# Moving twelve element-wise operations per border from VectorE to GpSimd in an encoder layer

## The chip, the cores and the metric

The kernel runs on one core of one Trainium2 chip. The metric is the device time of one execution in microseconds (us). The engines are named as the profile names them: PE (TensorE matmul), DVE (VectorE), ACT (ScalarE), POOL (GpSimd), SP (SyncE, which issues the loads).

## What is computed

Two sequences of 512 tokens with 1024 features go through one layer of a bidirectional encoder: pooling mixer and attention, a SwiGLU feed-forward network, and a gate for embeddings per layer. Two places matter here, and both have the same form: the hidden state is normed and multiplied by two large matrices or one.

```python
def rms_norm(x, g):
    y = x * rsqrt(mean(x * x, axis=-1) + EPS)
    return y * g
...
u2 = rms_norm(h, ln2)                                     # first border
h = h + (silu(u2 @ w_gate) * (u2 @ w_up)) @ w_down
gate = sigmoid(rms_norm(h, ple_norm) @ w_ple_gate)        # second border
return h + gate * (p @ w_ple_proj)
```

## The kernel before

Activations lie with features on the 128 partitions and the 512 tokens along the free axis, so one feature tile is a 128x512 block of float32. Every product is made of three passes over split operands: `split` (L128 to L133) makes the high part on ACT (L130) and the low part, source minus high part, on DVE or POOL (L133), and `mm3` (L155 to L159) issues high by high (L157), high by low (L158) and low by high (L159).

The two sequences s0 and s1 and the two halves of the features and of the outputs are the 2x2 blocks of a fast matrix product with seven products instead of eight (`seven`). Its seven activation operands are called B11, B21, T1, T2, T4, T3 and B22, four tiles each, and are used in this order. The seven weight operands are made on the fly by `stationary` (L649 on): SP loads raw weights, DVE adds and subtracts (L661), and ACT and DVE split. `fill` keeps up to eight such weights ahead, and SP's next load into a raw buffer waits until DVE has read the old one.

A border is the place where the normed hidden state becomes these operands. The first (gains at G_LN2) stands before the gate and up matrices, the second (G_PLE) before the gate of the embeddings; each begins with four products whose first step needs only B11 and B21. `norm_rows(..., False)` leaves the factors of the rows, `rb`, in a PSUM bank. `normed_first` makes B11 and B21 of s0. `normed_rest` (L765 to L786) does the rest from s1: x12 is the normed first half of s1, x22 its second half; T1 = x12 - x11 (L646), T2 = x22 - T1 (L776), T4 = x21 - T2 (L779), t3 = x22 - x12 (`difference`, L646), and then the pieces of B22 = x22 (L784) and of T3 = t3 (L786). `normed` makes one tile, on the engine that `eng` picks from the table TURNS by a name and an index i; x22 has i = 3:

```python
def normed(q, gc, k, rb, dst, i):                                        # L745
    if eng("norm", i) is nc.vector:
        nc.vector.scalar_tensor_tensor(dst, q.h[k], gcol(gc + k), rb[0], op0=ALU.mult, op1=ALU.mult)
    else:
        nc.scalar.activation(dst, q.h[k], AF.Copy, scale=gcol(gc + k))   # L749
        if len(rb) == 1:
            rb.append(Ft("rb"))
            nc.scalar.activation(rb[1], rb[0], AF.Copy)                  # L752
        nc.gpsimd.tensor_tensor(dst, dst, rb[1], op=ALU.mult)            # L753
```

So on DVE a tile is one instruction that reads `rb` in PSUM (L747); on POOL it is a scaled copy by ACT (L749) and a product of two operands in SBUF (L753), with one copy of `rb` from PSUM to SBUF for each border (L752). The bank of `rb` has the tag g, one of two; the products c and d (the tags of OB) take banks of that tag too, so the next c waits until the last reader of `rb` has ended. The order of the instructions on each engine is set by a scheduler from the order in the program, their dependences and its own estimates; each engine then works through its list in order. T3's pieces have the turn n5, those of B22 n4, the difference t3 the turn t3.

Of the kernel before, what the change touches and what calls it, by code (L numbers as in the profile page):

```python
# [60 lines left out]
    "hlo": "d",  # L61
    "wadd": "d",
    "wlo": "d",
    "norm": "d",
    "n0": "p",
    "n1": "p",
    "n2": "d",
    "n3": "d",
    "n4": "d",
    "n5": "d",  # L70
    "n6": "d",
    "tdif": "d",
    "t3": "d",
    "out": "d",
}
EMB = (1, 8, 4)
# [1030 lines left out]
```

## Time and profile before

| | us |
|---|---|
| median of 3 runs (1181.11 to 1186.27) | 1182.92 |
| the profiled execution, its own time | 1179.86 |
| its span in the trace | 1178.1 |

The span holds all instructions of the profiled execution; 1.76 us of its own time lie around it. The profiled execution is 3.06 us below the median. In the rows below, a row of the timeline is one instruction or several equal ones in a run (x8), with the start, the time from the first start to the last end, and in brackets the idle time of the engine ahead of it with what ended it. In the table by stretch, each engine has its busy time and, in brackets, its number of instructions; PEclk is the granted clock of PE as a share of the full 2.4 GHz.

### The profile page before, as it was taken

Reading aid. Unit: us, or ns where it says so; the run is one execution under the profiler, and the core shown is the slowest. Engines: PE = TensorE matmul, PEld = TensorE weight load, DVE = VectorE, ACT = ScalarE, POOL = GpSimd, SP = SyncE. Lnnn points to the kernel's source line nnn. Section 1 sums busy time; section 2 is a strip of 40 time slices with the busy share of each in tenths; the row PEclk is TensorE's granted clock in tenths of the full one; section 3 lists DMA queues with packets and bytes.
Section 4 is the critical chain, followed back from the end, with each engine's and each line's share of the span. In section 5 each row is a group of like instructions: output and inputs, shape, how many; then the busy total and the mean of one; then the engine's idle time right before and its main releaser. Section 6 shows DMA issues by size and latency. Waiting matters only on the chain.

```text
span 1178.1 us, 14952 instructions
## 1 busy us (share of the span) xinstructions
PE 1131.2 (96%) x5168; PEld 922.0 (78%) x5168; DVE 893.9 (76%) x1639; ACT 584.1 (50%) x1135; POOL 228.2 (19%) x290
## 2 busy tenths in 40 slices
PE   7999999998999989999999999999999999999997
PEld 7898756776778867888888888888778888887775
DVE  7377877778583789987768776787597867885997
ACT  7144478777562535655445454554332222345643
POOL 3533464746100220000000000000322212001200
PEclk9999999998999999999999999999999999999999
DMA  6211100102233521545244433544998475636045
GB/s 220 71 57 53 43 1 1 55 3 88 90 119 114 155 96 54 199 176 183 90 175 179 161 127 124 185 173 153 411 415 333 165 317 198 212 94 220 28 163 186
DMA packets 53644, 173.25 MB, mean 147 GB/s; under 512 B 6208, under 2 KB 6976, under 8 KB 53568
## 3 DMA queue, kind: packets, MB, share of 16 engines
q1 hardware_dynamic: 41328, 127.73, 32.3%
q0 software_dynamic: 12240, 44.57, 9.7%
q8 instruction: 40, 0.66, 0.2%
q14 instruction: 36, 0.29, 0.1%
HBM read 119.33 MB, written 52.95 MB: 146 GB/s over the span
## 4 chain that ended last, share of the span: by engine, by line
PE 81%; DVE 9%; issue 3%; POOL 3%; DMA 2%; ACT 2%; SPq 0%; DVEq 0%; ACTq 0%; POOLq 0%
PE a L158 8%; PE a L159 8%; PE a L157 8%; PE b L157 6%; PE b L158 6%; PE b L159 5%; PE s L523 4%; PE d L158 3%; PE d L159 3%; PE d L157 3%; PE o L157 2%; PE o L158 2%; PE o L159 2%; PE c L157 2%; PE c L158 2%
## 5 line engine op out<-in xcount | busy, mean ns | idle before, releaser
L130 ACT ACTIVATE w<-s 128x512 fp32r<-128x512 f32 (+2 forms) x168 | 96.8, 579 | 162.9 <-DVE s L661 61.5
L157 PE MATMUL a<-u,w 128*128 128x512 f32 x444 | 170.8, 390 | 2.9 <-DVE h L963 2.3
L158 PE MATMUL a<-u,w 128*128 128x512 f32 x444 | 172.9, 389 | 0.2 <-POOL u L133 0.2
L159 PE MATMUL a<-u,w 128*128 128x512 f32 x444 | 170.7, 389 | 0.0
L130 ACT ACTIVATE w<-raw 128x512 fp32r<-128x512 f32 (+2 forms) x126 | 70.8, 577 | 140.7 <-PE a L159 83.9
L133 DVE TENSOR_TENSOR w<-s,w 128x512 fp32r<-128x512 f32 (+2 forms) x168 | 103.8, 624 | 21.8 <-ACT w L130 21.3
L158 PE MATMUL b<-u,w 128*128 128x512 f32 x296 | 116.1, 393 | 4.3 <-DVE u L133 4.3
L157 PE MATMUL b<-u,w 128*128 128x512 f32 x296 | 115.9, 393 | 3.8 <-ACT w L130 2.1
L159 PE MATMUL b<-u,w 128*128 128x512 f32 x296 | 115.6, 392 | 0.0
L157 PEld LDWEIGHTS a<-u,w 128*128 128x128 f32 x444 | 83.2, 188 | 21.9 <-DVE h L963 2.7
L158 PEld LDWEIGHTS a<-u,w 128*128 128x128 f32 x444 | 83.3, 188 | 17.9 <-POOL u L133 0.6
L159 PEld LDWEIGHTS a<-u,w 128*128 128x128 f32 x444 | 83.3, 188 | 17.3
L133 DVE TENSOR_TENSOR w<-raw,w 128x512 fp32r<-128x512 f32 (+2 forms) x126 | 78.7, 637 | 21.1 <-ACT w L130 21.0
L942 POOL DMA_DIRECT2D u<-opT4p x11 | 6.2, 564 | 401.1 <-DVE s L661 363.8
L157 PEld LDWEIGHTS b<-u,w 128*128 128x128 f32 x296 | 56.0, 189 | 17.7 <-ACT w L130 2.9
L158 PEld LDWEIGHTS b<-u,w 128*128 128x128 f32 x296 | 55.9, 189 | 17.2 <-DVE u L133 5.6
L523 PE MATMUL s<-qkT 96*128 96x512 f32 x128 | 63.2, 596 | 2.8 <-ACT p L527 2.5
L159 PEld LDWEIGHTS b<-u,w 128*128 128x128 f32 x296 | 56.0, 189 | 11.5
L157 PE MATMUL c<-u,w 128*128 128x512 f32 x148 | 58.6, 399 | 5.0 <-DVE x L747 5.0
L159 PE MATMUL c<-u,w 128*128 128x512 f32 x148 | 58.4, 395 | 0.0
L158 PE MATMUL c<-u,w 128*128 128x512 f32 x148 | 58.3, 394 | 0.0
L158 PE MATMUL d<-u,w 128*128 128x512 f32 x148 | 57.7, 390 | 0.6 <-DVE u L133 0.6
(238 smaller groups left out, 2739.8 us busy)
## 6 DMA issues: line engine op xcount, KB each, us to landing
raw<-in_w_gate SPq DMA_DIRECT2D x24, 512.0 KB, 4.1
raw<-in_w_up SPq DMA_DIRECT2D x24, 512.0 KB, 3.6
raw<-in_w_down SPq DMA_DIRECT2D x24, 384.0 KB, 3.7
raw<-in_w_o SPq DMA_DIRECT2D x16, 512.0 KB, 3.6
raw<-in_w_pg SPq DMA_DIRECT2D x12, 512.0 KB, 3.7
opB11p<-st SPq DMA_DIRECT2D x11, 512.0 KB, 2.6
opB21p<-st SPq DMA_DIRECT2D x11, 512.0 KB, 3.7
opT1p<-st SPq DMA_DIRECT2D x11, 512.0 KB, 4.4
```

Source lines behind the costliest of these rows:

```text
L130: nc.scalar.activation(hi, src, AF.Copy)
L133: lo_eng.tensor_tensor(lo, src, hi.bitcast(F32), op=ALU.subtract)
L157: nc.tensor.matmul(ps, lhs[0], rhs[0], start=first, stop=False, skip_group_check=more)
L158: nc.tensor.matmul(ps, lhs[0], rhs[1], start=False, stop=False, skip_group_check=more)
L159: nc.tensor.matmul(ps, lhs[1], rhs[0], start=False, stop=last, skip_group_check=more)
L523: nc.tensor.matmul(ps, qT[:, tok(t)], kT, start=True, stop=True)
L942: nc.gpsimd.dma_start(d.bitcast(F32), spilled[k][f0 // 2 + j])
```

## The change

Three entries of the table TURNS change, and nothing else in the text of the kernel.

```diff
-    "norm": "d",
+    "norm": "dddp",
...
-    "n5": "d",
+    "n5": "p",
...
-    "t3": "d",
+    "t3": "p",
```

At each border four L747 (x22), four differences L646 (t3) and four low parts L133 (T3) leave DVE: twelve instructions. POOL gets twelve TENSOR_TENSOR: four products L753, four differences, four low parts. ACT gets four scaled copies L749 and one copy of `rb` L752. In all, DVE has 24 instructions fewer, POOL 24 more, ACT 10 more, and PE the same. The scheduler also sets the engines' lists anew around both borders, as the following rows show; names are those of the kernel with running numbers, so that u990 is the first piece of T1 at the first border, and td989 to td995 are the four T1.

DVE at the first border, before, from the last L747 on:

```order
L747 SCALAR_TENSOR_TENSOR x1988_4450<-h930_4088,gain_64,rb954_4200 128x512
L737 TENSOR_TENSOR x966_4346<-x966_4346,c967_4348 128x512
L133 TENSOR_TENSOR w978_4406<-s977_4404,w978_4406 128x512
L646 TENSOR_TENSOR td1005_4511<-x1985_4447 128x512
L646 TENSOR_TENSOR td989_4455<-x1985_4447,x0910_4011 128x512
L646 TENSOR_TENSOR td991_4460<-x1986_4448,x0911_4012 128x512
L646 TENSOR_TENSOR td993_4465<-x1987_4449,x0912_4013 128x512
L646 TENSOR_TENSOR td995_4470<-x1988_4450,x0913_4014 128x512
L646 TENSOR_TENSOR td1007_4516<-x1986_4448 128x512
L133 TENSOR_TENSOR w981_4425<-s980_4423,w981_4425 128x512
L879 TENSOR_TENSOR x966_4346<-x966_4346,x960_4309 128x512
L646 TENSOR_TENSOR td1009_4521<-x1987_4449 128x512
```

The same place now, behind four L747 instead of eight:

```order
L737 TENSOR_TENSOR x966_4346<-x966_4346,c967_4348 128x512
L133 TENSOR_TENSOR w978_4406<-s977_4404,w978_4406 128x512
L879 TENSOR_TENSOR x966_4346<-x966_4346,x960_4309 128x512
L646 TENSOR_TENSOR td989_4455<-x1985_4447,x0910_4011 128x512
L646 TENSOR_TENSOR td991_4460<-x1986_4448,x0911_4012 128x512
L646 TENSOR_TENSOR td993_4465<-x1987_4449,x0912_4013 128x512
L646 TENSOR_TENSOR td995_4470<-x1988_4450,x0913_4014 128x512
L133 TENSOR_TENSOR w981_4425<-s980_4423,w981_4425 128x512
L133 TENSOR_TENSOR u990_4457<-td989_4455,u990_4457 128x512
```

Before, the low part of the first piece of T1 (u990) stood two rows behind the last row shown; the differences t3 (td1005, td1007, td1009) that came ahead of it are gone from DVE, and it is now the last row of the second piece.

POOL at the first border, before, from the power that gives the row factors on; the loads of the down stage follow directly:

```order
L187 TENSOR_TENSOR r952_4193<-base951_4191,neghalf_67 128x4
L942 DMA u1563_7809<-opT4p0_4246 128x1024
L942 DMA u1564_7810<-opT4p1_4247 128x1024
L942 DMA u1565_7813<-opT3p0_4257 128x1024
```

And now:

```order
L187 TENSOR_TENSOR r952_4193<-base951_4191,neghalf_67 128x4
L753 TENSOR_TENSOR x1985_4447<-x1985_4447,rb997_4476 128x512
L753 TENSOR_TENSOR x1986_4448<-x1986_4448,rb997_4476 128x512
L753 TENSOR_TENSOR x1987_4449<-x1987_4449,rb997_4476 128x512
L753 TENSOR_TENSOR x1988_4450<-x1988_4450,rb997_4476 128x512
L646 TENSOR_TENSOR td1006_4517<-x1985_4447 128x512
L646 TENSOR_TENSOR td1008_4522<-x1986_4448 128x512
L646 TENSOR_TENSOR td1010_4527<-x1987_4449 128x512
L133 TENSOR_TENSOR u1014_4537<-td1006_4517,u1014_4537 128x512
L133 TENSOR_TENSOR u1015_4540<-td1008_4522,u1015_4540 128x512
L133 TENSOR_TENSOR u1016_4543<-td1010_4527,u1016_4543 128x512
L646 TENSOR_TENSOR td1012_4532<-x1988_4450 128x512
```

Eleven of the twelve new instructions are shown; they stand in one run, and the loads wait behind them.

DVE at the second border, before, from the last difference of T1 on (td2031), with the low parts of T1 (u2026 to u2032):

```order
L646 TENSOR_TENSOR td2031_10083<-x12024_10063,x01982_9867 128x512
L661 TENSOR_TENSOR s2013_10017<-raw2012_10015 128x512
L133 TENSOR_TENSOR u2026_10070<-td2025_10068,u2026_10070 128x512
L133 TENSOR_TENSOR u2028_10075<-td2027_10073,u2028_10075 128x512
L737 TENSOR_TENSOR x2018_10041<-x2018_10041,c2019_10043 128x512
L133 TENSOR_TENSOR u2030_10080<-td2029_10078,u2030_10080 128x512
L661 TENSOR_TENSOR s2016_10036<-s2013_10017,raw2011_10013 128x512
L646 TENSOR_TENSOR td2041_10124<-x12021_10060 128x512
L133 TENSOR_TENSOR u2032_10085<-td2031_10083,u2032_10085 128x512
```

And now (T1's low parts are u2027 to u2033, those of B22 u2044 to u2050):

```order
L646 TENSOR_TENSOR td2032_10089<-x12025_10069,x01983_9873 128x512
L133 TENSOR_TENSOR w2015_10025<-s2014_10023,w2015_10025 128x512
L133 TENSOR_TENSOR w2018_10044<-s2017_10042,w2018_10044 128x512
L737 TENSOR_TENSOR x2019_10047<-x2019_10047,c2020_10049 128x512
L133 TENSOR_TENSOR u2027_10076<-td2026_10074,u2027_10076 128x512
L133 TENSOR_TENSOR u2029_10081<-td2028_10079,u2029_10081 128x512
L133 TENSOR_TENSOR w2021_10062<-raw2013_10021,w2021_10062 128x512
L133 TENSOR_TENSOR u2044_10138<-x12022_10066,u2044_10138 128x512
L133 TENSOR_TENSOR u2031_10086<-td2030_10084,u2031_10086 128x512
L133 TENSOR_TENSOR u2033_10091<-td2032_10089,u2033_10091 128x512
L776 TENSOR_TENSOR td2026_10074<-x12022_10066,td2026_10074 128x512
L133 TENSOR_TENSOR u2046_10143<-x12023_10067,u2046_10143 128x512
```

Two low parts of weights (w2015, w2018) have come ahead of the first low part of T1, and the low parts of B22, which stood right behind the L747 before, have come in among those of T1 and the differences T2. On ACT at the same place the copy of `rb` for POOL stands behind the copy of a product's result and ahead of the next weights:

```order
L734 ACTIVATE x2019_10047<-a2016_10029 128x512
L752 ACTIVATE rb2034_10095<-rb1979_9868 128x512
L130 ACTIVATE w2018_10044<-s2017_10042 128x512
L999 ACTIVATE x2010_10004<-x2010_10004 128x512
L130 ACTIVATE u2027_10076<-td2026_10074 128x512
```

All four products L753 of the second border wait for that copy.

## Rows read from the trace of the kernel before

**Rows 1.** The profile page: busy time of the engines (part 1) and shares of the chain (part 4).
```profile
PE 1131.2 (96%) x5168; PEld 922.0 (78%) x5168; DVE 893.9 (76%) x1639; ACT 584.1 (50%) x1135; POOL 228.2 (19%) x290
...
PE 81%; DVE 9%; issue 3%; POOL 3%; DMA 2%; ACT 2%; SPq 0%; DVEq 0%; ACTq 0%; POOLq 0%
```

**Rows 2.** Waits of PE, 390 to 490 us: engine, line, releaser: total, times, longest us.
```profile
PE c L157 <- DVE x L747: 5.0, 1, 5.0
PE b L158 <- DVE u L133: 2.2, 1, 2.2
```

**Rows 3.** Waits of PE, 1100 to 1142 us.
```profile
PE b L158 <- DVE u L133: 2.1, 2, 1.3
...
PE d L158 <- DVE u L133: 0.6, 1, 0.6
```

**Rows 4.** Busy time by stretch: engines with instructions, granted PE clock, DMA share, GB/s.
```profile
440.00:450.00 10.00, 7.78 (x20) 5.76 (x20) 10.00 (x18) 2.82 (x5) 0.00 (x0) 0.67 0.00 0
1110.00:1120.00 10.00, 7.14 (x29) 4.91 (x28) 10.00 (x17) 6.41 (x12) 0.00 (x0) 1.00 0.00 0
```

**Rows 5.** Timeline of PE, 434 to 471 us: start, duration, engine, line, operation, idle before.
```profile
434.29 0.39 PE L159 MATMUL a<-u,w 128*128 128x512 f32 x1
439.66 0.76 PE L157 MATMUL c<-u,w 128*128 128x512 f32 x1 [4.99 <-DVE x L747]
...
444.55 0.63 PE L157 MATMUL b<-u,w 128*128 128x512 f32 x2
447.39 0.72 PE L158 MATMUL b<-u,w 128*128 128x512 f32 x1 [2.22 <-DVE u L133]
...
470.00 0.39 PE L158 MATMUL a<-u,w 128*128 128x512 f32 x1
470.22 0.39 PE L159 MATMUL a<-u,w 128*128 128x512 f32 x1
470.66 0.50 PE L157 MATMUL b<-u,w 128*128 128x512 f32 x1
```

**Rows 6.** Timeline of DVE, 434 to 471 us.
```profile
434.17 5.35 DVE L747 SCALAR_TENSOR_TENSOR x<-h,gain,rb 128x512 f32<-128x512 f32 x8
...
456.29 1.29 DVE L133 TENSOR_TENSOR u<-x,u 128x512 fp32r<-128x512 f32 x2
...
465.32 0.68 DVE L661 TENSOR_TENSOR s<-raw,s 128x512 f32<-128x512 f32 x1
...
470.32 0.69 DVE L661 TENSOR_TENSOR s<-raw 128x512 f32<-128x512 f32 x1 [1.30 <-DMA raw<-in_w_gate]
```

**Rows 7.** Timelines of DVE and POOL, 404 to 418 us.
```profile
404.49 5.36 DVE L747 SCALAR_TENSOR_TENSOR x<-h,gain,rb 128x512 f32<-128x512 f32 x8 [0.55 <-PE rb L205]
...
413.22 3.48 DVE L236 TENSOR_TENSOR sqh<-sqh,sq 128x512 f32<-128x512 f32 x2
...
405.98 11.88 POOL L133 TENSOR_TENSOR u<-x,u 128x512 fp32r<-128x512 f32 x8 [6.16 <-ACT u L130]
```

**Rows 8.** Timelines of DVE and POOL, 1086 to 1098 us.
```profile
1086.15 10.62 DVE L747 SCALAR_TENSOR_TENSOR x<-h,gain,rb 128x512 f32<-128x512 f32 x16 [6.24 <-PE rb L205]
...
1087.64 10.09 POOL L133 TENSOR_TENSOR u<-x,u 128x512 fp32r<-128x512 f32 x8 [12.35 <-ACT u L130]
```

**Rows 9.** Timelines of DVE and PE, 1102 to 1138 us.
```profile
1102.96 1.43 DVE L737 TENSOR_TENSOR x<-x,c 128x512 f32<-128x512 f32 x2 [1.67 <-PE c L159]
...
1135.18 0.69 DVE L661 TENSOR_TENSOR s<-raw 128x512 f32<-128x512 f32 x1
...
1111.72 0.50 PE L158 MATMUL b<-u,w 128*128 128x512 f32 x1 [1.32 <-DVE u L133]
...
1137.04 0.50 PE L157 MATMUL b<-u,w 128*128 128x512 f32 x1 [0.30 <-ACT w L130]
```

**Rows 10.** Groups of ACT by form: one count, busy us, mean ns, idle before.
```profile
L137 ACT ACTIVATE gx<-x,gain 128x512 fp32r<-128x512 f32 x16 | 10.7, 712 | 4.0 <-DMA x<-in_xT 4.0
...
L209 ACT ACTIVATE rb<-rb 128x512 f32<-128x512 f32 x2 | 1.2, 598 | 13.1 <-PE rb L205 13.1
```

## The prediction

> **What bounds the kernel now.** I read the page first: PE is busy 96% of the span and has 81% of the chain, DVE 76% and 9%, POOL 19% [rows 1]. So time is lost or won only where PE stands still or its next operand comes late, and these places are few. The waits of PE around the two borders show them. At the first border PE stands 5.0 us in front of a product c, until DVE's L747, and 2.2 us in front of the low part of T1's first piece [rows 2]; at the second it waits for low parts of T1 twice, 2.1 us in all, and 0.6 us for one of T4 [rows 3]. The table by stretch says why: DVE is busy 10.00 of 10 us in both stretches, while POOL runs nothing there and PE is busy 7.78 and 7.14 us [rows 4]. DVE is the bound at the borders, though not in the program. At the first border its backlog goes on until the add of two raw weights at 465.32; only then is the raw buffer free, the next load lands 4.3 us after that add's end (465.32 + 0.68 = 466.0 to 470.32), and DVE waits 1.30 us for it [rows 6]. PE has no slack there either: its rows follow each other by 0.22 us, but the one at 470.66 comes 0.44 us after its neighbour, at the change to a new product's weight [rows 5]. What comes later on DVE before 466 therefore comes later on PE behind 470. The second border has the same chain: DVE's first add of new raw weights at 1135.18, PE's wait of 0.30 us for a weight at 1137.04 [rows 9]. Behind each border PE runs without slack to the end, so a delay stays.
>
> **What leaves DVE.** One L747 takes 0.66 us in a row (10.62 / 16) [rows 8]; one TENSOR_TENSOR alone 0.60 us from start to start (two take 1.29, the last 0.69) [rows 6]. First border: 4 x 0.66 + 8 x 0.60 = 2.6 + 4.8 = 7.4 us less. Second border: the four L747 end before DVE's idle 1.67 us ahead of 1102.96 [rows 9] and gain nothing, so 8 x 0.60 = 4.8 us less. But the new order puts the four low parts of B22, which stood right behind L747 in front of that idle time, in among T1 and T2, where DVE has no free time: 4 x 0.60 = 2.4 us more. Left is 2.4 us less.
>
> **What comes to ACT.** Four scaled copies and one copy of rb, for which the nearest rows are 712 and 598 ns [rows 10]. ACT has slack at both borders (2.82 and 6.41 busy of 10 us [rows 4]), and I take nothing for them; without that cover it would be 4 x 0.7 + 0.6 = 3.4 us a border. The copy of rb sets one time. At the first border the fourth L747 ends at 434.17 + 2.64 = 436.8, and ACT comes to the copy behind three scaled copies and two weights, by my estimate near 437.6; it ends 0.6 us later, so the bank of rb is free at about 438.2 instead of 439.5 (434.17 + 5.35 [rows 6]), and c starts 1.3 us sooner.
>
> **What comes to POOL, and what it does to DVE.** Twelve TENSOR_TENSOR at 1.26 us (10.09 / 8 [rows 8]) are 15.1 us on an engine that is empty there [rows 4], and the loads queued behind them belong to the down stage, much later. The duration is no cost, the company is. Beside L747, which reads rb in PSUM, eight POOL rows take 10.09 us and sixteen L747 their usual 0.66 us [rows 8]: neither slows the other. But eight of the same POOL rows take 11.88 us at the first border, where DVE turns from L747 to rows with two operands in SBUF, and two of these DVE rows take 3.48 us instead of 1.29 [rows 7]. So DVE loses (3.48 - 1.29) / 2 = 1.10 us for each POOL row it runs beside, and starts one row per 0.60 + 1.10 = 1.70 us. All that DVE runs behind L747 at the borders is of that kind, except adds of a product in PSUM (L737). Before, POOL is silent there; now it runs twelve such rows against DVE's backlog. I take 1.10 us for each of the twelve: 13.2 us a border. Bounds: nothing, if they only meet PSUM rows or idle time; 1.26 us each, if DVE stands for the whole POOL row.
>
> The Trainium skill (SBUF — State Buffer, section Who interferes with whom) makes the second bound the rule: a VectorE instruction with two SBUF inputs and a GpSimd instruction that reads SBUF exclude each other, and the second to issue stands until the first has finished. Agreed is who slows whom. The size is not: by the rule as an estimate from the rows it is 12 x 1.26 = 15.1 us a border, and the sum would be 3.8 us higher than the one here.
>
> **The sum.** First border: +13.2 - 7.4 = +5.8 us. Walked through the list: four products L753 and three differences occupy POOL from 438.3 to about 450; DVE's four T1 at one per 1.70 us end near 445.5, a weight near 447, and the low part of u990 near 449, so PE's wait of 2.2 us for it grows to about 5 although c came sooner; the low parts of T3 hit DVE again from 460 on, and the raw buffer is free about 5.4 us late. Second border: +13.2 - 2.4 = +10.8 us. There the copy of rb stands late in ACT's list, so that the products L753 start near 1110, just when T1's low parts are due; two low parts of weights now stand ahead of them too, and PE's wait at 1111.72 [rows 9] grows by 6 to 7 us. Together +16.6 us: 1179.86 + 16.6 = 1196.5 us for an execution like the profiled one. That stands 3.06 us below the median of the runs, so the median goes to 1182.92 + 16.6 = **1199.5 us**. If only ten of twelve POOL rows meet DVE's, it is 4.4 us less (1195.1); with whole rows lost it is 3.8 us more (1203.3).
>
> **Rivals.** *The backlog goes (faster).* If POOL's rows mostly pass DVE by, the change does what its text says: DVE is relieved, c comes 1.3 us sooner, and the waits for low parts, 2.2, 2.1, 0.6 and 0.3 us [rows 2, 3, 9], go: 6.5 us, 1176.4 us. It decides by a count: break-even is 7.4 / 1.10 = 6.7 colliding rows at the first border and 2.4 / 1.10 = 2.2 at the second. For it: at the first border DVE runs the first of its rows while POOL waits for rb. Against it: DVE has no free time for the 20 us in which POOL's rows run. Chance 0.06. The Trainium skill (Perfetto Trace Analysis, section Optimizing Scalar/DVE Operations) says that moving work off a saturated VectorE may make sense and warns that it might not help between these two engines; rows 7 bear out the warning.
>
> *About half collide (same).* Six of twelve: 6.6 - 7.4 = -0.8 and 6.6 - 2.4 = +4.2 us, together +3.4: 1186.3 us. For it: of the eight POOL rows of 11.88 us only some four can have been held up, (11.88 - 10.09) / (1.70 - 1.26) = 4 [rows 7, 8], so a longer alternation is not shown. Against: those four are the ones beside which DVE had such rows. Chance 0.13.
>
> *PE's clock falls too (worse).* Behind the gap of 5 us the twelve matmuls of c took 444.55 - 439.66 = 4.9 us where 12 x 0.23 = 2.7 is usual [rows 5], and the granted clock was 0.67 in that stretch [rows 4], so part of it at the lower level, 1.2 GHz. Behind the waits of 1.3 us and less it stayed at 1.00 [rows 4]. If each of the three or four longer gaps that I forecast costs 2.2 us this way and DVE does not make that time good, it is 7 to 9 us more: some 1208 us. Chance 0.11. That the change does not do what it says I exclude: the lists show all twelve rows on POOL at each border.
>
> **How the numbers follow.** Forecast 0.70 (1195 to 1203), same 0.13, faster 0.06, worse 0.11. 0.5% is 5.9 us, about what a measurement here can tell from no change: under 1177.0 or over 1188.8. Slower by more: 0.70 + 0.11 and a little of the case of half = 0.82; faster 0.05; within 0.13. The range goes from 1186 (half collide) to 1208.
>
> **What would show it.** In the profile after: DVE rows of 1.6 to 1.8 us behind L747 at both borders, alternating with POOL; PE's wait for u's low part (L133) near 449 and near 1118 longer, 5 and 7 us instead of 2.2 and 1.3; that for c shorter, by 1.3 us; the load that landed at 470.32 near 476. If DVE's rows stay at 0.69 us there, or POOL's rows stretch instead, I am wrong and the time falls; if DVE's rows stretch but PE's rows behind 470 are not later, the chain to the weights has slack that I do not see.

## The result and the profile after

The changed kernel took 1200.86 us (median of 4 runs, 1198.39 to 1202.19) against 1184.35 us for the kernel before (4 runs): slower by 16.5 us. The ratio on record is 1.0161 (95% interval 1.0136 to 1.0185); the two medians alone give 1.0139, inside it, so the loss is known to some 3 us and no better. The forecast was 1199.5 us and +16.6. The profiled execution took 1198.39 us with a span of 1196.6; 18.5 us of span were added to that of the profiled execution before.

Where they were added can be read by numbering PE's rows, of which both kernels have 5168, and comparing the start of row n in both. Ahead of the first border the changed kernel is 0.36 us early (median of rows 1960 to 2019), behind it 5.57 us late (rows 2145 to 2199), ahead of the second 6.35 us late (rows 4780 to 4849), behind it 19.19 us late (rows 5090 to 5159). So the first border costs 5.9 us, the second 12.8, and what lies between 0.8; behind PE's last row the tail is 0.7 us shorter. This measure, "border 1" and "border 2" below, is free of what one execution does elsewhere.

The page first, busy times of the engines (before: [rows 1]):

```profile
PE 1136.5 (95%) x5168; PEld 923.5 (77%) x5168; DVE 899.6 (75%) x1615; ACT 590.1 (49%) x1145; POOL 279.7 (23%) x314
```

POOL has 51.5 us more busy time for 24 rows that take 1.26 us alone, 30.2 us together. DVE, with 24 rows fewer, has 5.7 us more. The waits of PE at the first border and then at the second (before: [rows 2, 3]):

```profile
PE a L158 <- DVE u L133: 3.6, 1, 3.6
PE c L157 <- DVE x L737: 3.3, 1, 3.3
PE b L158 <- DVE u L133: 1.7, 1, 1.7
PE a L157 <- ACT u L130: 1.2, 1, 1.2
```

```profile
PE b L158 <- DVE u L133: 8.5, 1, 8.5
PE a L157 <- ACT x L734: 4.2, 1, 4.2
```

The wait for c is 1.7 us shorter. It now ends with DVE's L737 and no longer with L747, four of which are gone ahead of it. New are a wait for T2's low part (a L158, 3.6 us) and, at the second border, 8.5 us for T1's low part and 4.2 us for an ACT copy. Two of PE's rows at the first border:

```profile
455.99 0.79 PE L158 MATMUL a<-u,w 128*128 128x512 f32 x1 [3.61 <-DVE u L133]
...
475.84 0.50 PE L157 MATMUL b<-u,w 128*128 128x512 f32 x1 [0.87 <-ACT w L130]
```

DVE there, start and length of its rows:

```profile
438.59 2.49 DVE L646 TENSOR_TENSOR td<-x,x 128x512 f32<-128x512 f32 x4
...
441.60 0.68 DVE L133 TENSOR_TENSOR u<-td,u 128x512 fp32r<-128x512 f32 x1
442.23 0.69 DVE L737 TENSOR_TENSOR x<-x,c 128x512 f32<-128x512 f32 x1
442.84 2.86 DVE L133 TENSOR_TENSOR u<-td,u 128x512 fp32r<-128x512 f32 x2
445.62 1.77 DVE L133 TENSOR_TENSOR w<-raw,w 128x512 fp32r<-128x512 f32 x1
447.31 1.74 DVE L133 TENSOR_TENSOR u<-td,u 128x512 fp32r<-128x512 f32 x1
448.98 1.77 DVE L776 TENSOR_TENSOR td<-x,td 128x512 f32<-128x512 f32 x1
450.67 1.80 DVE L879 TENSOR_TENSOR x<-x,x 128x512 f32<-128x512 f32 x1
...
466.20 1.77 DVE L661 TENSOR_TENSOR s<-raw,raw 128x512 f32<-128x512 f32 x1 [2.43 <-POOL u L133]
...
474.43 0.69 DVE L661 TENSOR_TENSOR s<-raw 128x512 f32<-128x512 f32 x1
```

And POOL there:

```profile
438.22 10.29 POOL L753 TENSOR_TENSOR x<-x,rb 128x512 f32<-128x512 f32 x4 [11.12 <-ACT rb L752]
448.47 5.12 POOL L646 TENSOR_TENSOR td<-x 128x512 f32<-128x512 f32 x3
458.68 8.74 POOL L133 TENSOR_TENSOR u<-td,u 128x512 fp32r<-128x512 f32 x3 [5.09 <-ACT u L130]
```

The four T1 differences run at the usual 0.60 us, and u's first low part is done at 442.3: up to there DVE is not held. It is POOL that stands: its four products take 10.29 us instead of 5.0, and single rows show that the first took 5.23 us, until DVE came to a row with an operand in PSUM (L737 at 442.23). From then on both alternate, and DVE's rows take 1.74 to 1.80 us. The same again at 458.68: three low parts in 8.74 us, of which the first had 6.24, until DVE stopped at 463.77. It stopped because the sum of raw weights at 466.20 waited 2.43 us for the second of these low parts, which came behind the first and ended at 466.16: t3's four buffers and the sums share the tag G. The load that landed at 470.32 now lands at 474.43 [rows 6].

The second border goes the other way round. POOL, then DVE:

```profile
1116.30 6.78 POOL L753 TENSOR_TENSOR x<-x,rb 128x512 f32<-128x512 f32 x4 [11.16 <-ACT rb L752]
1123.05 5.09 POOL L646 TENSOR_TENSOR td<-x 128x512 f32<-128x512 f32 x3
1136.58 8.98 POOL L133 TENSOR_TENSOR u<-td,u 128x512 fp32r<-128x512 f32 x3 [8.44 <-DVE u L133]
```

```profile
1115.64 0.68 DVE L737 TENSOR_TENSOR x<-x,c 128x512 f32<-128x512 f32 x1
1116.24 5.71 DVE L646 TENSOR_TENSOR td<-x,x 128x512 f32<-128x512 f32 x4
1121.88 3.46 DVE L133 TENSOR_TENSOR w<-s,w 128x512 fp32r<-128x512 f32 x2
...
1125.86 2.84 DVE L133 TENSOR_TENSOR u<-td,u 128x512 fp32r<-128x512 f32 x2
...
1144.38 1.73 DVE L661 TENSOR_TENSOR s<-raw,raw 128x512 f32<-128x512 f32 x1 [2.44 <-POOL u L133]
```

Here POOL's first product comes while DVE still works on a PSUM row (L737 at 1115.64), gets in, and from then on DVE's T1 differences take 5.71 us for four and T1's low parts start only at 1125.86. PE shows what it costs, with the granted clock beside it:

```profile
1117.83 0.73 PE L157 MATMUL b<-u,w 128*128 128x512 f32 x2 [1.35 <-ACT u L130]
1127.07 0.79 PE L158 MATMUL b<-u,w 128*128 128x512 f32 x1 [8.51 <-DVE u L133]
...
1148.46 0.79 PE L157 MATMUL a<-u,w 128*128 128x512 f32 x1 [4.17 <-ACT x L734]
```

```profile
450.00:460.00 10.00, 5.23 (x14) 3.44 (x12) 10.00 (x13) 6.95 (x13) 4.91 (x4) 0.59 0.00 1
1120.00:1130.00 10.00, 2.93 (x7) 2.35 (x8) 10.00 (x10) 3.76 (x7) 8.14 (x5) 0.54 0.00 0
1148.46:1151.50 3.04, 3.04 (x7) 2.46 (x8) 3.04 (x4) 1.15 (x3) 1.09 (x1) 0.50 0.65 198
```

Two stretches of 10 us now run at 0.59 and 0.54 of the full clock (before, one at 0.67 [rows 4]); PE had stood still 3.6 and 8.5 us in them. Behind the wait of 4.17 us seven rows run at 0.50.

### The profile page after: what moved, and what is told of

Its sections match the earlier page's. It is cut to its first block, busy times and chain, and to the rows that moved or that the text cites. A ratio compares the mean times of both kernels' runs of the same rounds, so it can differ in the third digit from the quotient of the medians.

```text
span 1196.6 us, 14969 instructions
## 1 busy us (share of the span) xinstructions
PE 1136.5 (95%) x5168; PEld 923.5 (77%) x5168; DVE 899.6 (75%) x1615; ACT 590.1 (49%) x1145; POOL 279.7 (23%) x314
## 4 chain that ended last, share of the span: by engine, by line
PE 81%; DVE 6%; issue 5%; POOL 3%; DMA 2%; ACT 2%; SPq 0%; DVEq 0%; ACTq 0%; POOLq 0%
PE a L157 8%; PE a L158 8%; PE a L159 8%; PE b L157 5%; PE b L159 5%; PE b L158 5%; PE s L523 4%; PE d L158 3%; PE d L159 3%; PE d L157 3%; PE o L157 2%; PE o L158 2%; PE o L159 2%; PE y L550 2%; PE c L157 2%
## 5 line engine op out<-in xcount | busy, mean ns | idle before, releaser
L158 PE MATMUL a<-u,w 128*128 128x512 f32 x444 | 174.7, 393 | 3.8 <-DVE u L133 3.6
L158 PE MATMUL b<-u,w 128*128 128x512 f32 x296 | 116.4, 393 | 10.3 <-DVE u L133 10.2
L133 DVE TENSOR_TENSOR w<-s,w 128x512 fp32r<-128x512 f32 (+2 forms) x168 | 106.3, 636 | 26.4 <-ACT w L130 25.8
L157 PEld LDWEIGHTS a<-u,w 128*128 128x128 f32 x444 | 84.1, 190 | 29.3 <-ACT x L734 4.6
L158 PEld LDWEIGHTS a<-u,w 128*128 128x128 f32 x444 | 84.4, 190 | 22.3 <-DVE u L133 4.2
L159 PEld LDWEIGHTS a<-u,w 128*128 128x128 f32 x444 | 84.3, 190 | 17.7
L133 DVE TENSOR_TENSOR w<-raw,w 128x512 fp32r<-128x512 f32 (+2 forms) x126 | 79.8, 646 | 23.2 <-ACT w L130 23.2
L158 PEld LDWEIGHTS b<-u,w 128*128 128x128 f32 x296 | 56.1, 189 | 23.5 <-DVE u L133 12.0
L963 DVE TENSOR_TENSOR h<-h,a 128x512 f32<-128x512 f32 x64 | 42.2, 683 | 25.9 <-PE a L159 25.9
L158 PE MATMUL c<-u,w 128*128 128x512 f32 x148 | 58.1, 393 | 0.0
```

Of the source, the lines that this page charges most:

```text
L133: lo_eng.tensor_tensor(lo, src, hi.bitcast(F32), op=ALU.subtract)
L157: nc.tensor.matmul(ps, lhs[0], rhs[0], start=first, stop=False, skip_group_check=more)
L158: nc.tensor.matmul(ps, lhs[0], rhs[1], start=False, stop=False, skip_group_check=more)
L159: nc.tensor.matmul(ps, lhs[1], rhs[0], start=False, stop=last, skip_group_check=more)
L963: nc.vector.tensor_tensor(h, h, ps, op=ALU.add)
```

## The experiments

Theory A is the prediction's: a POOL row beside DVE rows with two SBUF operands costs DVE time. Rival B puts the loss on t3 and T3, which come late from POOL and hold buffers and ACT's list. Rival C says that POOL's rows cost by being late whatever they read, rival D that DVE does not bound the borders at all.

"Stretched" is the sum over DVE's TENSOR_TENSOR rows longer than 0.85 us at a border (from 425 and from 1085 us on) of what they have above 0.68 us, with the number of such rows; the kernel before has 0 and 0.9 (1). All ratios are to the kernel before on the same chip, with 95% intervals.

| kernel | ratio | border 1, us | border 2, us | stretched 1 | stretched 2 |
|---|---|---|---|---|---|
| the change | 1.0161 (1.0136 to 1.0185) | +5.9 | +12.8 | 10.3 (10) | 10.2 (10) |
| e_norm | 1.0063 (1.0042 to 1.0084) | +2.1 | +7.2 | 3.7 (4) | 4.3 (4) |
| e_t3n5 | 1.0093 (1.0062 to 1.0124) | +3.8 | +7.4 | 4.4 (4) | 4.9 (5) |
| e_inplace | 1.0223 (1.0192 to 1.0255) | +11.8 | +10.4 | 10.4 (11) | 10.2 (10) |
| b_inplace | 1.0052 (1.0035 to 1.0069) | +1.6 | +2.7 | 0 | 0.9 (1) |
| e_single | 1.0057 (1.0037 to 1.0078) | +1.0 | +7.7 | 4.1 (10) | 3.3 (8) |
| e_early | 1.0094 (1.0065 to 1.0123) | +5.6 | +4.7 | 7.3 (7) | 14.2 (15) |
| e_early_norm | 1.0029 (1.0014 to 1.0043) | -0.7 | +3.7 | 1.7 (2) | 7.3 (7) |
| e_tdif | 0.9984 (0.9971 to 0.9997) | -3.0 | +1.8 | 0 | 5.3 (5) |
| e_left | 0.9931 (0.9912 to 0.9950) | -5.7 | -0.9 | 0 | 3.8 (4) |
| e_tdif1 | 0.9981 (0.9963 to 0.9999) | -2.9 | 0.0 | 0 | 0.9 (1) |

**e_norm: the norm alone**

```diff
-    "norm": "d",
+    "norm": "dddp",
```

> Only the norm of x22 goes to POOL (four products L753 a border, with ACT's copies); t3 and T3's low parts stay on DVE. Theory A (each POOL row beside DVE rows with two SBUF operands costs DVE 1.10 us): first border 4 x 1.10 - 4 x 0.66 = +1.8 us, second +4.4 us (its L747 lay before idle time), +6 us in all against the kernel before, ratio 1.005. Theory B (the loss comes from DVE and ACT waiting for POOL's late t3 and T3 rows, through t3's buffers and ACT's order): 0 or a small gain, -3 to +1 us.

Measured +7.4 us (1188.52 against 1181.14), border 1 +2.1, border 2 +7.2. Theory A had +1.8 and +4.4; B had about none. Four rows are stretched at each border, one for each product, as A says. The 2.8 us over A at border 2 are the subject of e_early_norm.

**e_t3n5: t3 and T3's low parts alone**

```diff
-    "n5": "d",
+    "n5": "p",
...
-    "t3": "d",
+    "t3": "p",
```

> Only t3 and T3's low parts go to POOL (eight rows a border); x22 is normed on DVE as before. Theory A: 8 x 1.10 - 8 x 0.60 = +4.0 us a border, +8 us, ratio 1.007. Theory B: most of the whole change's loss, +12 to +16 us, ratio 1.010 to 1.014, with DVE idle 2 us and more in front of a sum of raw weights (L661) that waits for POOL's u, at both borders.

Measured +12.0 us (1193.14 against 1181.14), which is B's lower end; the interval, 7.3 to 14.6 us, takes in A's +8 too. Border 1 gives +3.8 where A had +4.0, but not in A's way: A reckoned with eight stretched rows, and four are stretched, 4.4 us against the 4.8 us that leave DVE. What did come is B's sign, DVE idle 2.42 us in front of L661 for POOL's u, and PE waits 2.5 us for a weight at 478.36. Border 2 costs more. POOL there:

```profile
1124.10 9.50 POOL L646 TENSOR_TENSOR td<-x 128x512 f32<-128x512 f32 x1 [7.85 <-DVE w L133]
1133.56 3.75 POOL L133 TENSOR_TENSOR u<-td,u 128x512 fp32r<-128x512 f32 x3
```

One difference stood 9.50 us: from 1124.5 to 1132.4 DVE ran 13 rows with two SBUF operands without a break. DVE then stood still itself, 3.7 us in front of L661 <- POOL u, and PE 6.2 us in front of an ACT copy. So both theories hold a part: DVE loses where POOL gets in, and where it does not, its results are late.

**e_inplace and b_inplace: no buffer of G for t3**

```diff
-            t3.append(difference(x22[j], x12[j], eng("t3", j), "G"))
+            eng("t3", j).tensor_tensor(x12[j], x22[j], x12[j], op=ALU.subtract)
+            t3.append(x12[j])
```

> The change, but t3 is written over x12 and takes no buffer of the tag G, which the sums of raw weights use too. Against b_inplace (the same edit on the kernel before). Theory A: the twelve collisions a border stay, so e_inplace is 13 to 17 us above b_inplace. Theory B: DVE's idle 2.4 us for POOL's u in front of L661 is gone at both borders and the weights come early; e_inplace is at most 6 us above b_inplace and 8 to 14 us below the change.

> The kernel before with t3 written over x12, so that the sums of raw weights wait for no buffer of t3. Both theories: DVE does the same work, but the scheduler can put the sums that free the raw buffers some 20 us earlier at each border, so the load that DVE waits 1.30 us for at 470.32 and PE's 0.2 to 0.3 us for weights go: 0 to -5 us against the kernel before.

e_inplace lies 1.0223 / 1.0052 = 1.7%, some 20 us with an uncertainty of 4, over b_inplace; A had 13 to 17, B at most 6. It lies above the change, where B had it 8 to 14 us below. DVE's wait for POOL's u in front of L661 is gone, and PE waits for POOL directly; POOL's four low parts take 15 us:

```profile
PE a L158 <- DVE u L133: 5.9, 1, 5.9
PE a L158 <- POOL u L133: 4.9, 1, 4.9
```

```profile
460.80 15.05 POOL L133 TENSOR_TENSOR u<-x,u 128x512 fp32r<-128x512 f32 x4 [3.89 <-ACT u L130]
```

So the shared tag G is where the lateness came out, not what made it. b_inplace was missed: +6.3 us instead of a gain. The sums of raw weights did come earlier on DVE, at 439.88 for one that stood at 465.32, and with them work on weights ahead of T1 and T2. But the borders show only +1.6 and +2.7 us of it, and 1.7 come back between them; 5.8 us come behind both, with a wait that the kernel before does not have:

```profile
1170.27 0.50 PE L157 MATMUL b<-u,w 128*128 128x512 f32 x1 [3.57 <-ACT x L734]
```

I read it as the scheduler's new order; that is not shown. e_inplace has a wait of this kind too (2.3 us), and by the borders alone the pair differs by 10.3 and 7.6 us.

**e_single: one operand for POOL's rows**

```diff
-            nc.gpsimd.tensor_tensor(dst, dst, rb[1], op=ALU.mult)
+            nc.gpsimd.tensor_scalar(dst, rb[1], 1.0, None, op0=ALU.mult)
...
-        e.tensor_tensor(d, x, y, op=ALU.subtract)
+        if e is nc.gpsimd:
+            e.tensor_scalar(d, x, 1.0, None, op0=ALU.mult)
+        else:
+            e.tensor_tensor(d, x, y, op=ALU.subtract)
...
+        if name == "T3":
+            nc.scalar.activation(d[:, 0, :], src, AF.Copy)
+            nc.gpsimd.tensor_scalar(d[:, 1, :], d[:, 0, :].bitcast(F32), 1.0, None, op0=ALU.mult)
```

> The change with its twelve POOL rows a border made TENSOR_SCALAR with one operand (the product takes rb alone, t3 takes x22 alone, the low part takes the high part alone), so the operands x22, T3 and B22 hold other numbers; order and dependences stay much as in the change. Theory A (DVE's rows with two SBUF operands and POOL's rows with two exclude each other): DVE's rows behind L747 start every 0.60 us again, no POOL row is held for 5 us, and DVE has 7.4 and 2.4 us less work: 3 to 8 us below the kernel before. Theory C (POOL's rows cost by being late and by the order of the lists, whatever they read; any POOL row that reads SBUF holds DVE): 8 us or more above the kernel before.

Measured +6.6 us (1187.86 against 1181.31; the interval is 4.4 to 9.2): A's condition, two operands on POOL, falls, and C's 8 us or more is only just reached by the interval. A POOL row with one SBUF operand holds up DVE's rows too, and for less time (the edit shifts the line numbers: L760 is the product of L753, L653 the difference of L646):

```profile
438.31 12.53 POOL L760 TENSOR_SCALAR x<-rb 128x512 f32<-128x512 f32 x4 [10.63 <-ACT rb L759]
```

```profile
438.68 2.49 DVE L653 TENSOR_TENSOR td<-x,x 128x512 f32<-128x512 f32 x4
...
447.96 1.09 DVE L783 TENSOR_TENSOR td<-x,td 128x512 f32<-128x512 f32 x1 [1.38 <-POOL x L760]
```

DVE's stretched rows take 1.09 us here, 0.41 us more than usual, where they take 1.75 beside POOL's rows with two operands; 0.41 x 24 is 9.8 us, 1.10 x 24 would be 26.4. And POOL's four products take 12.53 us, the first 5.42, so that DVE itself stands 1.38 us at 447.96 for the product that its own run of rows had kept out. The Trainium skill (SBUF — State Buffer, section Who interferes with whom) says that a VectorE instruction with two SBUF inputs contends with a GpSimd instruction that reads SBUF, and that the order of issue decides who blocks. The first is what these rows show. The second they show only in part: POOL's second product took 4.22 us from 443.71 to 447.93, while four DVE rows that started behind it (444.09 to 445.90) ran at their usual length.

With the same twelve POOL rows, but shorter collisions, border 1 falls from +5.9 to +1.0 us. Border 2 stays at +7.7 us with only 3.3 us stretched. PE's idle time there is 2.8 us more than in the kernel before, and its rows take 4.9 us longer: behind two waits of 2.5 us they run at half the clock, the first time as follows.

```profile
1114.40:1120.00 5.60, 5.59 (x13) 4.43 (x14) 5.60 (x8) 2.18 (x4) 5.60 (x5) 0.50 0.00 0
```

So the clock has a share at this border that DVE's rows do not show.

**e_early and e_early_norm: the products moved to a free place**

```diff
+        for j in range(HALF):
+            normed(s1, gc, j + HALF, rb, x22[j], 3)
         t = []
...
-            normed(s1, gc, j + HALF, rb, x22[j], 3)
...
-    rb = [norm_rows(norm_columns(s1.sq), False)]
+    rb = copied([norm_rows(norm_columns(s1.sq), False)])
...
     rb = [[norm_rows(c, False)] for c in r]
+    copied(rb[1])
```

`copied` is L752 at once. e_early_norm has the same edit with only the norm on POOL.

> The change with the same twelve POOL rows a border, but rb copied by ACT as soon as it is made and x22 scaled ahead of T1, so that the four products run while DVE still reads PSUM (L747, L737) at the first border and while DVE has idle time at the second. Theory A: four of the twelve collisions a border go, 4 x 1.10 x 2 = 9 us below the change, +6 to +9 us against the kernel before. Theory B (the loss hangs on t3 and T3, late on POOL): at most 4 us below the change, +12 us or more against the kernel before.

> Only the norm of x22 on POOL (as e_norm), with rb copied early and x22 scaled ahead of T1. Theory A: no collision is left at the first border and DVE has four L747 less, 0 to -4 us against the kernel before, and 7 to 11 us below e_norm. Theory C: as e_norm, +5 us or more.

e_early: 1.0094 against the change's 1.0161, 8 us less (5 us by the medians of the change), with an uncertainty of some 4.5, so that it does not tell A's 9 from B's 4; it is 12.2 us above the kernel before (1193.55 against 1181.31), where A had 6 to 9. By PE's rows the gain is all at border 2 (+4.7 for +12.8), where rb's copy had come late. At border 1 nothing was gained: the last product and a t3 difference that the scheduler pulled up met T1's differences, four of which took 4.77 us.

Nor did the collisions go at border 2. There e_early has 14.2 us of stretched rows against the change's 10.2 and yet costs 8 us less: 5.0 us of them fall between 1102 and 1111, ahead of T1, where DVE of the change stood idle, 9.3 us in all between 1100.5 and 1113.8. So the sum of the stretched rows is not the price; a row stretched into idle time need not cost PE anything.

e_early_norm: 1.0029 against e_norm's 1.0063, 4 us less, where A had 7 to 11, and still 2.9 us above the kernel before (1184.25 against 1181.31). Border 1 came out even a little earlier (-0.7 for +2.1). At border 2 the products now stand ahead of low parts of B11 and B21 in POOL's list, and those alternate with DVE (7.3 us stretched): the collisions were moved rather than removed. A has the right sign, and a size that only holds where the place moved to is really free.

**e_left: the twelve rows left out**

```diff
-            if len(rb) == 1:
-                rb.append(Ft("rb"))
-                nc.scalar.activation(rb[1], rb[0], AF.Copy)
-            nc.gpsimd.tensor_tensor(dst, dst, rb[1], op=ALU.mult)
...
-        e.tensor_tensor(d, x, y, op=ALU.subtract)
+        if e is nc.gpsimd:
+            nc.scalar.activation(d, x, AF.Copy)
+        else:
+            e.tensor_tensor(d, x, y, op=ALU.subtract)
...
+        if name == "T3":
+            nc.scalar.activation(d[:, 0, :], src, AF.Copy)
+            nc.scalar.activation(d[:, 1, :], src, AF.Copy)
```

> The change with its twelve POOL rows a border left out: x22 stays scaled by the gains alone, t3 is a copy of x22 by ACT, and T3's low part a copy by ACT, so those operands hold other numbers; DVE's list is the one of the change, ACT has eight rows a border more and no copy of rb. It shows what the relief of DVE is worth when no POOL row stands beside it. Theory A: the waits of PE for c and for T1's low parts shrink, DVE's rows start every 0.60 us: 4 to 9 us below the kernel before, ratio 0.992 to 0.997, and some 20 us below the change. Theory D (DVE is not what bounds the borders: the new order of the lists and ACT's added rows cost the time): above the kernel before.

Measured -7.9 us (1172.84 against 1180.76): A. DVE's first border and PE's waits there:

```profile
439.44 2.49 DVE L653 TENSOR_TENSOR td<-x,x 128x512 f32<-128x512 f32 x4
...
447.27 1.89 DVE L779 TENSOR_TENSOR td<-x,td 128x512 f32<-128x512 f32 x3
```

```profile
437.87 0.62 PE L157 MATMUL c<-u,w 128*128 128x512 f32 x1 [2.44 <-DVE x L754]
...
443.19 0.50 PE L158 MATMUL b<-u,w 128*128 128x512 f32 x1 [0.29 <-DVE u L133]
...
449.81 0.50 PE L158 MATMUL a<-u,w 128*128 128x512 f32 x1 [0.87 <-DVE u L133]
```

The waits of 5.0 and 2.2 us [rows 2] are 2.4 and 0.3. So DVE's load does bound the first border, and taking the rows off it is worth 8 us; having POOL do them costs 1.0161 - 0.9931 = 2.3%, 27 us with an uncertainty of some 4 (25 us by the medians of the change, 26 by the spans), or some 1.1 us for each of the 24 rows. DVE's stretched rows come to 20.5 us in the change; how the 27 us divide into them and POOL's late results is not shown. Its DVE list at border 1 is that of the change up to the last difference of T4. This pair shows that the loss comes with POOL's work and not with the lists that lack the rows on DVE, and rules out D. At border 2 e_left gains only 0.9 us. It has 3.8 us stretched of its own, as low parts of B11 and B21 on POOL meet DVE's rows there, but DVE stands idle 2.07 us for c right behind them, so they are not what keeps the gain small; PE still waits 1.4 and 1.1 us for parts of T1.

**e_tdif and e_tdif1: another move, into the PSUM rows**

```diff
-    "tdif": "d",
+    "tdif": "pdd",
```

In e_tdif1 it holds for the first border alone.

> The kernel before with one other move: the four differences T1 = x12 - x11 of each border on POOL. At the first border they run while DVE reads PSUM in the last L747, at the second while DVE has idle time. Theory A: no collision at the first border, four rows of 0.60 us less for DVE at each, -2 to -5 us against the kernel before. Theory C: POOL's 1.26 us a row delay T1, +2 us or more.

> The kernel before with T1's four differences on POOL at the first border alone, where they run while DVE reads PSUM in its last L747. In e_tdif the first border came out 3.0 us earlier and the second 1.8 us later by the starts of PE's rows. Theory A: 2 to 4 us below the kernel before, ratio 0.997 to 0.998; if the order set by the scheduler decides instead of the collisions, no difference.

```profile
434.64 4.97 POOL L646 TENSOR_TENSOR td<-x,x 128x512 f32<-128x512 f32 x4 [7.50 <-DVE x L747]
```

```profile
433.82 5.35 DVE L747 SCALAR_TENSOR_TENSOR x<-h,gain,rb 128x512 f32<-128x512 f32 x8
...
442.10 0.68 DVE L133 TENSOR_TENSOR u<-td,u 128x512 fp32r<-128x512 f32 x1
```

Four POOL rows in 4.97 us beside L747 at its usual 5.35 us: nothing is held, T1's first low part is done at 442.8, where PE's row that needed it had come at 447.39 [rows 5], and border 1 comes out 3.0 us earlier, just above the 2.4 us that four rows are worth. At border 2 the same four rows meet the low parts of B22 (5.3 us stretched) and it comes out 1.8 us later. e_tdif measures 1180.07 against 1181.31 us, e_tdif1 1177.44 against 1180.76: 0.9984 and 0.9981, both intervals just below 1. A found the place; the gain of 2 us is near what can be measured. e_tdif1 has the lowest ratio of the complete kernels here, 0.2% under the kernel before (0.01 to 0.37%), though not to be told from e_tdif.

## Why the prediction was right, and where not

**What bounds the kernel.** Both borders carry all but 0.8 us of the difference, and at the first e_left shows that DVE's load is what PE waits for. The chain to the weights was misread. PE's row of 470.66 starts when ACT's copy of a product ends (470.01 + 0.59), and the weight that comes from the load of 470.32 is split only at 471.44, behind that row:

```profile
470.01 0.59 ACT L734 ACTIVATE x<-b 128x512 f32<-128x512 f32 x1
...
471.44 1.17 ACT L130 ACTIVATE w<-s 128x512 fp32r<-128x512 f32 x2
```

So these rows do not show a chain without slack. In the changed kernel PE's rows just ahead of that number are 4.4 us late already. They went there from 6.0 us early by the waits of 1.7, 1.2 and 3.6 us for T1's and T2's parts and some 2.9 us in rows at the lower clock. The wait of 0.87 us for a weight at 475.84, after a load that came 4.1 us later (474.43), goes with the last 1.2 us.

**What leaves DVE.** 7.4 and 2.4 us were taken. By PE, e_left gives 5.7 at border 1 and 0.9 at border 2.

**What comes to ACT.** c did come sooner, at 437.62 for 439.66, but not by the way forecast. It started with the end of DVE's L737 (436.79 + 0.68), ahead of the end of the copy of rb at 438.14.

**What POOL does to DVE.** The term was 12 x 1.10 a border. Ten rows were stretched at each border, 10.3 and 10.2 us: 1.03 us a row, not the 1.26 of the upper bound, and ten rows of twelve, the case named with the sum. What I did not have is the other side: where DVE was in a run of such rows, POOL was kept out for 5 us and more. My walk through the first border had DVE held from 438.3 on and T1's first low part near 449; it was done at 442.3, and PE's long wait came one operand later, at 455.99, for T2.

**The sum.** Border 1: predicted +5.8, measured +5.9, from terms that were both too large: -5.7 + 10.3 = +4.6. The remaining 1.3 us would fit POOL's late results, for which DVE stood idle 2.43 us; no run prices them alone. Border 2: predicted +10.8, measured +12.8, and there DVE's rows do not add up to it. PE's own do: its idle time grows by 10.3 us, above all by the 8.51 in front of 1127.07 and the 4.17 in front of 1148.46, and its rows take 2.6 us longer, 1.5 of them in the seven rows at half the clock behind 1148.46. DVE's 2.44 us in front of 1144.38 are not part of it, as PE waits for no weight behind that. The copy at 1148.46 was ready to run but stood in ACT's list behind a piece of t3:

```profile
1147.29 0.63 ACT L130 ACTIVATE u<-td 128x512 fp32r<-128x512 f32 x1 [5.89 <-POOL td L646]
1147.83 0.58 ACT L734 ACTIVATE x<-a 128x512 f32<-128x512 f32 x1
```

That piece was late because three low parts ahead of it on POOL took 8.98 us, the first of them 6.51. So the step that failed is the price of a POOL row that is kept out: it was taken as nothing. Two other terms were too large, the twelve collisions (ten) and the relief (5.7 and 0.9 us for 7.4 and 2.4). That +16.6 met +16.5 is in part luck, as these errors covered each other. Right at the second border was what POOL does when it gets in first: PE's wait of 1.32 us grew by 7.2, where 6 to 7 was said.

**The rivals.** "The backlog goes" has its mechanism shown by e_left, 8 us, and fails on its condition: 20 rows collide. "About half collide" is out: ten of twelve. "PE's clock falls too" did happen. At border 1 the slow rows lie ahead of the wait for a weight, which PE would have reached sooner and stood in front of longer; that is argued, no run shows it. At border 2 no wait follows the seven slow rows behind 1148.46, so their 1.5 us are part of the loss, and in e_single slow rows make most of border 2. No run prices the clock alone.

**What would show it.** Seen as said: DVE rows of 1.74 to 1.80 us, c sooner, the load later (474.43; 476 was said), PE's wait for T1 at the second border longer (8.5 us). Not seen: alternation from the first row on at border 1, and a wait of 5 us for T1 near 449 (1.7 us at 449.11). And POOL's rows did stretch, to 5.23, 6.24 and 6.51 us, which was named as a sign that the time falls; it did not fall, because their results were then late.

## What to carry to other kernels

Before moving element-wise rows from DVE to POOL, list what DVE runs beside them: beside rows that read PSUM they cost nothing (e_tdif, border 1), beside rows with two SBUF operands each that got in cost DVE 1.0 to 1.1 us here, against the 0.6 us that the move saved. What of that reaches PE depends on what DVE does behind it: 14.2 us of stretched rows, a third of them in what had been idle time, cost 4.7 us (e_early, border 2). A saturated DVE can gain from losing work (8 us in e_left); given to POOL, the rows need a stretch that is really free, and moving them earlier without checking what else lies there moves the collisions. And look for what takes a buffer or a place in a list behind a moved row, since a POOL row that is kept out comes out somewhere else, here in the weights' sums and in ACT's copies.

## What was not expected of the hardware

A run of DVE rows with two SBUF operands keeps a waiting POOL row out until the run breaks, by a PSUM row or by idle time, not for one row alone: 5.23 us over the six rows that start from 438.59 to 441.60, 9.50 us over thirteen. Once POOL is in, its TENSOR_TENSOR rows and DVE's alternate one for one at about 1.70 us. POOL rows with a single SBUF operand (e_single) are kept out too, 5.42 and 4.22 us, and cost less when they are in: every second or so of DVE's rows is longer, by 0.41 us instead of some 1.07.
